# All low parts of the experts' weight slices on VectorE, and the selection mask by eight 16-bit comparisons

## The chip, the cores and the metric

The kernel runs on one core of a Trainium2 chip. Its metric is the device time of one execution in microseconds (us), as a median over runs. The engines are TensorE (PE in the profile; PEld is its weight load), VectorE (DVE), ScalarE (ACT), GpSimd (POOL) and SyncE (SP), which issues most of the DMA transfers.

## What is computed

One layer of a network over 1024 tokens of 1024 channels: a token mixer (gated delta rule in both directions and pooling), a projection, and then a mixture of experts, after which the result is normalised. The change lies almost wholly in the mixture of experts. It has 16 experts; each takes the 128 tokens that have the largest affinity to it, and puts them through three matrices of 1024 x 1024 in 32-bit floats (201 MB in all):

```python
def expert_choice_ffn(h, w_router, w_gate, w_up, w_down):
    B_, L, D = h.shape
    cap = EC_CAPACITY * L // N_EXPERTS                       # 128
    aff = jax.nn.softmax((h @ w_router).astype(jnp.float32), axis=-1)
    top_aff, top_idx = lax.top_k(jnp.swapaxes(aff, 1, 2), cap)
    xe = jax.vmap(lambda hb, ib: hb[ib])(h, top_idx)
    hid = jax.nn.silu(jnp.einsum('becd,edf->becf', xe, w_gate)) * jnp.einsum('becd,edf->becf', xe, w_up)
    ye = jnp.einsum('becf,efd->becd', hid, w_down) * top_aff[..., None].astype(h.dtype)
    combine = lambda ib, yb: jnp.zeros((L, D), yb.dtype).at[ib.reshape(-1)].add(yb.reshape(-1, D))
    return jax.vmap(combine)(top_idx, ye)
```

## The kernel before

A product of 32-bit matrices is made on TensorE from two parts of each operand: a high part, which is the operand rounded to the narrower format that TensorE multiplies in (fp32r), and a low part, which is what the rounding left. Three products are summed: high by high, high by low, low by high.

**Slices.** A weight matrix is taken in slices of 128 rows by 1024 columns (512 KB), eight to a matrix and 384 in all. The list `seq` sets the order in which they are needed: after the first gate matrix, for each expert e its up matrix, the gate matrix of expert e + 1, and its down matrix. These 24 slices are called a cycle here. SyncE loads slices into a ring of 34 places (tiles `rawa`, `oa`, `rawb`); a place takes its next slice once its present one has been split.

**Splitting.** `split_slice` (L1503 to L1517) makes the two parts of the next slice of the list: ScalarE copies it to the high part `fhi` (L1513), and then VectorE or GpSimd subtracts the high part from it and writes the low part `flo` (L1514). There are four buffers for each part. `use_slice` issues the six matmuls of a slice (L1632: two halves of 512 columns by three products, the low part's in the middle), and then calls `split_slice` for the slice four further on. Which engine makes the low part is a rule on the slice's number i: GpSimd where i % 6 is 5 (four slices of a cycle), VectorE otherwise. The first four slices are split on GpSimd in an earlier stage, beside the search for the experts' thresholds; that is not touched.

**A cycle in the code.** `up_mm(e)` uses the eight slices of the up matrix. After the fourth, `transpose_split` makes the next expert's input: eight transposes on TensorE (L1668), the high part on ScalarE (L1670, tiles `lhs`), the low part on VectorE (L1671). After the eighth, `select(e + 2)` finds which tokens an expert takes: eight small matmuls with that expert's mask (L1644), four small operations on VectorE (L1648 to L1652: `sv`, `ix`, `af`, `af`); `gather` issues an indirect DMA from GpSimd (L1658, tile `xe`), which lands the rows for the expert after next; and `onehot(e + 3)` makes the next mask (L1614). Then VectorE multiplies the activated gate by the up products (L1726, tile `sg`). `gate_mm(e + 1)` uses four slices, `transpose_split` transposes `sg`, and `gate_mm` uses the other four. `down_mm(e)` uses eight, and `scatter(e)` weights the result on VectorE (L1736, `ye`) and adds it to the output in DRAM by an indirect DMA from GpSimd (L1738, `accd`).

Each engine runs its instructions in the order in which the code issues them.

**The mask.** For each of eight tiles of 128 tokens, `oh[:, t, :]` holds a one where a token (a partition) has a slot (a column, 1 to 128) of the expert. `posT[:, t, e]` is a token's slot for expert e, or 0. One comparison over 8 x 128 elements makes it from two 32-bit operands, both broadcast. The mask itself is in 16 bits (bf16). The first mask is made from a tile in PSUM and the others from `posT`.

**A constant.** `slots` (the numbers 1 to 128 on each partition) is made on GpSimd ahead of the output projection, in a row of other constants; behind them GpSimd has a small operation for the output's norm (L1080, `ro`), whose result VectorE needs (L1082).

Of the kernel before, what the change touches and what calls it, by code (L numbers as in the profile page):

```python
# [7 lines left out]
F32 = mybir.dt.float32  # L8
F32R = mybir.dt.float32r
BF16 = mybir.dt.bfloat16  # L10
# [10 lines left out]
NT = 8  # L21
# [31 lines left out]
def trunk_kernel(ctx, tc, x, c, ctxt, c_ctx, w_mod, b_mod, norm1, norm2, w_in, conv_w, a_log, dt_bias,  # L53
# [12 lines left out]
    # ---------------------------------------------------------------- constants  # L66
# [17 lines left out]
    # parameter rows -> per-partition columns  # L84
# [13 lines left out]
    # inverse window sizes of the box means along rows and columns  # L98
# [14 lines left out]
    # ---------------------------------------------------------------- modulation and normalised inputs  # L113
# [97 lines left out]
    def prefetch(load=True):  # L211
        """split the next column block, then load the one after"""
        i = pos[0]
        pos[0] += 1
        if i < len(cols):
            split[i] = w_split(*cols[i])
        if load and i + 1 < len(cols):
            w_load(*cols[i + 1])
# [40 lines left out]
    def more_gemv():  # L259
        """the rest of the modulation, in steps"""  # L260
        for i, b in enumerate(MG):
            yield from gemv_steps(b, PSK, lambda: PSK.tile([128, 4, 128], F32, name="gtp"))
            if i + 2 < len(MG):
                gemv_load(MG[i + 2])
            if i < 2:
                yield
# [3 lines left out]
    # tokens: first in xnT, how many, first in their own part, row of the modulation, their part  # L270
    GROUPS = {"x": (LC, L, 0, 0, hx), "A": (LC, 512, 0, 0, hx), "B": (LC + 512, 512, 512, 0, hx), "c": (0, LC, 0, 1, hc)}
    # for four of the eight channel tiles, the steps of the modulated inputs: in place as they are (a), and as two
    # parts, high (h, or H from what is in place) and low (l, by DVE or POOL)
# [22 lines left out]
    # ---------------------------------------------------------------- input projection, convolution, pooling  # L296
# [5 lines left out]
    def project_ab(ks):  # L302
        """the decay and step columns, four parts of the sum side by side (32 columns each)"""
        if not ab_px:
            ab_px.extend(PSK.tile([128, 512], F32, name=f"ab{t}") for t in range(2))
            ab_px.append(PS2.tile([128, 4, 128], F32, name="tp").rearrange("p a b -> p (a b)")[:, 0:LC])
        for dst, n in zip(ab_px, (LC, LC + 512, 0)):
            m = dst.shape[1]
            for k in ks:
                j = k % 4  # L310
                PE.matmul(dst[32 * j:32 * j + 32], wab[:, k, :], xnT[:, k, n:n + m], start=(k < 4), stop=(k >= 4),
                          tile_position=(0, 32 * j))
# [14 lines left out]
    # [tile, channel, gate heads and pool groups, token]  # L327
# [4 lines left out]
    def delta_setup():  # L332
        """decays and step sizes of all chunks"""
# [56 lines left out]
    def copy2(t, dst, src):  # L390
        """two halves on two engines"""
        if t:
            DVE.tensor_copy(dst, src)
        else:
            ACT.activation(dst, src, AF.Copy)
# [3 lines left out]
    def rows_tile(ct, i):  # L399
        """where group i of a channel tile's tokens is transposed"""  # L400
# [6 lines left out]
    def conv_post(ct, px, pc, dst, after):  # L407
        """convolution and silu of channel tile ct, then what follows; in steps"""
# [103 lines left out]
    # keep the array's clock up until the first of these inputs is there  # L512
# [3 lines left out]
    # the products of the first block of keys as their inputs come: with the high parts (h), with the low parts (l)  # L516
# [39 lines left out]
    # eg[:, 0]: decay up to a token, 1: from it to the chunk's end, 2: of the whole chunk  # L556
# [35 lines left out]
    # ---------------------------------------------------------------- v and q; the chunks' inverses of the delta rule  # L592
# [8 lines left out]
    def masked_decays(cj):  # L601
        """log decays of the chunk's tokens in the columns of the tokens that they act on"""
# [11 lines left out]
    # a chunk's inverse ([lane][direction]) and decays on their way to DRAM  # L614
# [14 lines left out]
    def prep(cj, lane):  # L629
        """inverse and masked scores of chunk cj (0, 1: context) for both directions"""  # L630
# [118 lines left out]
    def k_scales():  # L749
        """step sizes over the keys' squared norms, once these are known"""  # L750
# [9 lines left out]
    def advance_preps():  # L760
        """the next stage of one of the chunks' inverses that are under way"""
# [40 lines left out]
    def pool_post(g, px):  # L802
        """difference to the box mean, mixed within the group"""
# [65 lines left out]
    # ---------------------------------------------------------------- gated delta rule, both directions  # L869
    OA = pools.push("oa")  # L870
    # the tiles in the order of their output projection, two to a buffer, which then holds experts' weights
# [25 lines left out]
    def scores(cj):  # L897
        """masked, decayed products of the chunk's queries and keys"""
# [11 lines left out]
    def scan(cjs, is_first, last):  # L910
        """one step of both directions: chunk cjs[d] for direction d"""
# [7 lines left out]
        def mm(lhs, rhs):  # L919
            """four products, one per head"""  # L920
            p = sc()
            for h in range(H):
                PE.matmul(p[:, h, :], lhs(h), rhs(h), start=True, stop=True)  # L923
            return p
# [104 lines left out]
    # ---------------------------------------------------------------- parts of the output projection, some ahead of it  # L1029
# [3 lines left out]
    def alt(t):  # L1033
        """tiles in turn use the buffers of two pools"""
# [17 lines left out]
    def wo_split(k):  # L1052
        """the parts of a block of rows times the gate"""
# [62 lines left out]
    def prefetches():  # L1116
        """what the output projection needs first, between the steps of the delta rule"""
# [50 lines left out]
    # ---------------------------------------------------------------- output projection, gated residual, router  # L1168
# [7 lines left out]
    # the order in which the experts' weights are needed: (expert, gate / up / down); the last but one's down after  # L1176
    # the last one's up
# [8 lines left out]
    # slices that for once lie in places of other tiles, loaded once the ring is full  # L1186
# [8 lines left out]
    def ring_b():  # L1195
        """the ring's places that the stage before frees last come last"""
# [47 lines left out]
    def y_mm(t, ks, hfs=(0, 1)):  # L1244
        """the last tile's halves lie in buffers of their own"""
# [13 lines left out]
    def residual(t, hf=None):  # L1259
        """x1 = x + y; the gate is in y's weights"""  # L1260
# [6 lines left out]
    def x1_norm(t, part=None):  # L1267
        """1 / rms; for one half of the columns after the other, or all at once"""
# [39 lines left out]
    def router_last(t, ks):  # L1308
        """the last tile's, on shorter a way"""
# [20 lines left out]
    def ffn_input(t):  # L1330
        """modulated input of the experts; x1 starts the sum of their outputs"""
# [16 lines left out]
    # partition (t, e) -> same expert; earlier tiles of the same expert  # L1348
# [11 lines left out]
    # search for the threshold: of each three candidates the first two, and for ScalarE the third one's negative plus  # L1360
    # half a unit, above the first value; their changes from digit to digit; the steps; the limits' negatives
# [18 lines left out]
    # token number and affinity (three exact parts) of every token  # L1380
# [10 lines left out]
    POOL.iota(slots, pattern=[[1, 128]], base=1, channel_multiplier=0, allow_small_or_imprecise_dtypes=True)  # L1391
    late = []
    for i in range(NT):
        t = [ORDER[j] if 0 <= j < NT else None for j in (i, i + 1, i + 2, i - 1)]
        if i == 0:
# [7 lines left out]
            # what the last tiles need lies where the next stage's first loads don't go  # L1403
# [86 lines left out]
    # ---------------------------------------------------------------- expert choice: the CAP largest per expert  # L1490
# [9 lines left out]
    # the places of what is needed late lie where the last stage's tiles are  # L1500
# [4 lines left out]
    def split_slice(eng=None):  # L1505
# [8 lines left out]
        (eng or (POOL if i % 6 == 5 and 5 < i < NS - 4 else DVE)).tensor_tensor(lo, raw, hi.bitcast(F32), op=OP.subtract)  # L1514
# [18 lines left out]
    # the threshold's bits, two at a time: bits 29..16, then bits 15..0 of the values that share them  # L1533
# [12 lines left out]
    def search(key, dst, nxt, unit, n):  # L1546
        """largest first + i * unit (i < 4 ** n) that at least CAP keys of the expert reach; the keys are multiples of unit

        of each three candidates, ScalarE counts for the last one the keys above less the keys below; nxt has them
        without the last digit's share d"""  # L1550
# [37 lines left out]
    # all above the threshold, and as many of the equal ones, from the first token on, as there is room for  # L1588
# [23 lines left out]
    def onehot(e, pos=None):  # L1612
        oh = FE.tile([128, NT, 128], BF16, name="oh", bufs=1)
        DVE.tensor_tensor(oh, slots[:, None, :].to_broadcast([128, NT, 128]),  # L1614
                          (posT if pos is None else pos)[:, :, e:e + 1].to_broadcast([128, NT, 128]), op=OP.is_equal)
# [6 lines left out]
    # ---------------------------------------------------------------- experts  # L1622
# [38 lines left out]
    def transpose_split(src, e):  # L1661
        """the two parts of a transposed operand of expert e; its input's and its hidden one's share buffers"""
# [33 lines left out]
    def transpose_onehot(e):  # L1696
        """the expert's selection with the slots on the partitions"""
# [71 lines left out]
    # ---------------------------------------------------------------- the last expert's outputs and the final norm  # L1769
# [12 lines left out]
    def final_sum(t):  # L1782
        """the last expert's outputs on top of the others'; TensorE adds some tiles', VectorE the others'"""
# [61 lines left out]
```

## Time and profile before

| | |
|---|---|
| median of 3 runs | 1383.76 us (1383.68 to 1389.02) |
| span of the profiled execution, first to last instruction | 1383.9 us |
| TensorE matmuls busy | 1260.0 us, 91% of the span |
| VectorE busy | 1020.7 us, 74% |
| ScalarE busy | 750.0 us, 54% |
| GpSimd busy | 564.1 us, 41% |
| DMA | 328.39 MB, mean 237 GB/s |

The profile is of one execution. It gives that execution's span and no time outside it, so the span is read as its own time; it is 0.1 us from the median. The shares are averages over stages with different limits, so what a change in the experts' stage is worth is read from that stage: from about 760 us to 1356 us, of which nearly all is a repetition of the cycle described above.

### The profile page before, as it was taken

How to read it: one execution, taken by the hardware profiler on the slowest of the kernel's cores; microseconds unless marked ns; L12 is line 12 of the kernel's file. 1: busy time of each engine (PE TensorE's matmuls, PEld its weight loads, DVE VectorE, ACT ScalarE, POOL GpSimd, SP SyncE). 2: the span in 40 equal slices, each digit the busy share in tenths (PEclk: the TensorE clock that was granted, in tenths of full speed). 3: DMA queues.
4: the chain of work that ended last, by engine and by line, in shares of the span. 5: the costliest groups of instructions: out<-in, count | busy, mean ns of one | idle time of the engine just before them, and what ended most of it. 6: DMA issues, size and time to landing. Idle time of an engine off the chain costs nothing.

```text
span 1383.9 us, 26524 instructions
## 1 busy us (share of the span) xinstructions
PE 1260.0 (91%) x10355; PEld 994.4 (72%) x10355; DVE 1020.7 (74%) x1606; ACT 750.0 (54%) x1103; POOL 564.1 (41%) x455
## 2 busy tenths in 40 slices
PE   5899898989999989989952999999999999999997
PEld 3476777766767779978842777777777777777884
DVE  4763675575775446845667889999999999999885
ACT  5443433343433335233232777777777777777783
POOL 5701543494845125651152333434334434443332
PEclk9999999999999999999975999999999999999999
DMA  9657213212223278436793899999999999999806
GB/s 355 211 195 257 69 37 101 73 48 79 73 68 108 78 262 302 168 129 223 260 342 128 282 310 365 363 371 370 363 364 367 366 363 369 367 368 358 322 3 256
DMA packets 140760, 328.39 MB, mean 237 GB/s; under 512 B 13517, under 2 KB 53082, under 8 KB 140634
## 3 DMA queue, kind: packets, MB, share of 16 engines
q1 hardware_dynamic: 134826, 305.72, 60.8%
q0 software_dynamic: 5376, 19.40, 5.4%
q8 instruction: 81, 1.33, 0.4%
q10 hardware_dynamic: 432, 1.57, 0.3%
q14 instruction: 45, 0.37, 0.1%
HBM read 287.32 MB, written 39.32 MB: 236 GB/s over the span
## 4 chain that ended last, share of the span: by engine, by line
PE 61%; DVE 18%; issue 8%; POOL 4%; DMA 4%; ACT 3%; SPq 0%; DVEq 0%; POOLq 0%; ACTq 0%
PE pd L1632 12%; PE pu L1632 11%; PE px L484 11%; DVE flo L1514 6%; PE y L1256 6%; PE pg L1632 5%; PE sc L923 4%; PE iv L687 2%; DVE acc L428 2%; PE tp L1668 1%; DVE sg L1726 1%; DMA wm<-in_w_mod_dram 1%; PE gv L132 1%; ACT fhi L1513 1%; DMA Vd<-rows 1%
## 5 line engine op out<-in xcount | busy, mean ns | idle before, releaser
L1514 DVE TENSOR_TENSOR flo<-rawb,fhi 128x1024 fp32r<-128x1024 f32 x147 | 207.4, 1457 | 26.4 <-ACT fhi L1513 26.2
L484 PE MATMUL px<-hx,whi 128*128 128x512 f32 x640 | 221.0, 425 | 4.5 <-ACT hx L290 2.7
L1513 ACT ACTIVATE fhi<-rawb 128x1024 fp32r<-128x1024 f32 x176 | 186.0, 1061 | 65.2 <-PE pg L1632 31.7
L1514 DVE TENSOR_TENSOR flo<-rawa,fhi 128x1024 fp32r<-128x1024 f32 x133 | 184.0, 1428 | 26.5 <-ACT fhi L1513 25.4
L1513 ACT ACTIVATE fhi<-rawa 128x1024 fp32r<-128x1024 f32 x158 | 166.9, 1061 | 60.0 <-PE pg L1632 32.0
L1632 PE MATMUL pg<-fhi,lhs 128*128 128x512 f32 x544 | 157.7, 402 | 0.0
L1632 PE MATMUL pu<-fhi,lhs 128*128 128x512 f32 x512 | 146.7, 398 | 0.0
L484 PEld LDWEIGHTS px<-hx,whi 128*128 128x128 f32 x640 | 112.7, 192 | 39.6 <-issue 11.3
L1514 POOL TENSOR_TENSOR flo<-rawb,fhi 128x1024 fp32r<-128x1024 f32 x29 | 75.6, 2606 | 144.7 <-ACT fhi L1513 78.0
L1632 PE MATMUL pd<-fhi,lhs 128*128 128x512 f32 x480 | 134.2, 396 | 0.0
L1514 POOL TENSOR_TENSOR flo<-rawa,fhi 128x1024 fp32r<-128x1024 f32 x29 | 74.8, 2581 | 134.3 <-ACT fhi L1513 65.4
L484 PE MATMUL px<-hx,wlo 128*128 128x512 f32 x320 | 128.5, 402 | 0.0
L1632 PEld LDWEIGHTS pg<-fhi,lhs 128*128 128x128 f32 x544 | 100.5, 189 | 22.5 <-ACT lhs L1670 0.4
L1632 PEld LDWEIGHTS pu<-fhi,lhs 128*128 128x128 f32 x512 | 95.0, 188 | 21.8
L1632 PEld LDWEIGHTS pd<-fhi,lhs 128*128 128x128 f32 x480 | 90.1, 188 | 21.6
L1632 PE MATMUL pg<-flo,lhs 128*128 128x512 f32 x272 | 87.2, 402 | 15.7 <-DVE flo L1514 15.7
L201 POOL TENSOR_TENSOR wlo<-wraw,whi 128x1024 fp32r<-128x1024 f32 x16 | 40.1, 2503 | 125.8 <-ACT whi L200 125.8
L1632 PE MATMUL pu<-flo,lhs 128*128 128x512 f32 x256 | 80.5, 395 | 0.0
L1256 PE MATMUL y<-ohi,mx 128*128 128x512 f32 x256 | 76.0, 402 | 0.8 <-DVE oa L981 0.8
L1632 PE MATMUL pd<-flo,lhs 128*128 128x512 f32 x240 | 75.5, 396 | 0.0
L1632 PEld LDWEIGHTS pg<-flo,lhs 128*128 128x128 f32 x272 | 50.3, 189 | 32.7 <-DVE flo L1514 21.4
L484 PEld LDWEIGHTS px<-hx,wlo 128*128 128x128 f32 x320 | 61.5, 192 | 14.1
(454 smaller groups left out, 2471.4 us busy)
## 6 DMA issues: line engine op xcount, KB each, us to landing
rawb<-in_w_down_dram SPq DMA_DIRECT2D x61, 512.0 KB, 8.0
rawb<-in_w_gate_dram SPq DMA_DIRECT2D x58, 512.0 KB, 5.5
rawb<-in_w_up_dram SPq DMA_DIRECT2D x57, 512.0 KB, 6.3
rawa<-in_w_gate_dram SPq DMA_DIRECT2D x56, 512.0 KB, 5.6
rawa<-in_w_up_dram SPq DMA_DIRECT2D x54, 512.0 KB, 5.7
rawa<-in_w_down_dram SPq DMA_DIRECT2D x52, 512.0 KB, 7.0
wm<-in_w_mod_dram SPq DMA_DIRECT2D x48, 512.0 KB, 6.7
wraw<-in_w_in_dram SPq DMA_DIRECT2D x20, 512.0 KB, 4.6
```

The lines of the kernel that those rows point to most:

```text
L132: PE.matmul(ps[32 * j:32 * j + 32], cs[:, k, :], t[:, i, :], start=(q < 2), stop=(q >= 2), tile_position=(0, 32 * j))
L201: (POOL if pos[0] > 4 else DVE).tensor_tensor(lo[:, :, :n], raw[:, :, :n], hi[:, :, :n].bitcast(F32), op=OP.subtract)
L428: DVE.scalar_tensor_tensor(acc, pad[:, j:j + L], convw(j, ct), acc, op0=OP.mult, op1=OP.add)
L484: PE.matmul(dst, wp[:, k, :], src[hp][:, k, o], start=start and i == 0, stop=stop and i == len(parts) - 1)
L687: PE.matmul(iv[r, u, o:64], pa[r, u, :], PV[r, u, o:64], start=True, stop=True)
L923: PE.matmul(p[:, h, :], lhs(h), rhs(h), start=True, stop=True)
L1256: PE.matmul(ys[t, hf][:, hf, :], l_[:, k, :], r_[:, 512 * hf:512 * hf + 512], start=(k == KORD[0] and i == 0), stop=(k == KORD[-1] and i = ...
L1513: ACT.activation(hi, raw, AF.Copy)
L1514: (eng or (POOL if i % 6 == 5 and 5 < i < NS - 4 else DVE)).tensor_tensor(lo, raw, hi.bitcast(F32), op=OP.subtract)
L1632: PE.matmul(ps[:, hf, :], l_[:, k, :], r_[:, 512 * hf:512 * hf + 512], start=(k == 0 and n == 0), stop=(k == KD - 1 and n == 2))
L1668: PE.transpose(tp[:, q, :], src[:, 128 * k:128 * k + 128], ident)
L1726: DVE.tensor_tensor(gs[e], gs[e], pu.pop(e).rearrange("p a b -> p (a b)"), op=OP.mult)
```

## The change

Three edits. In `split_slice` the rule that gives every sixth low part to GpSimd is taken out, so that VectorE makes all of them. In `onehot` the one comparison of 8 x 128 elements becomes eight comparisons of 128 elements, each of a 16-bit copy of the slot numbers with one 32-bit number per partition (the first mask stays as it was). The 16-bit copy, `slotb`, is a new tile and one more operation on GpSimd. The rest of the full diff takes comments and docstrings out.

```diff
     slots = WS.tile([128, 128], F32, name="slots")
     POOL.iota(slots, pattern=[[1, 128]], base=1, channel_multiplier=0, allow_small_or_imprecise_dtypes=True)
+    slotb = WS.tile([128, 128], BF16, name="slotb")
+    POOL.tensor_copy(slotb, slots)
...
         if i >= SPLITS:
             ACT.activation(hi, raw, AF.Copy)
-        (eng or (POOL if i % 6 == 5 and 5 < i < NS - 4 else DVE)).tensor_tensor(lo, raw, hi.bitcast(F32), op=OP.subtract)
+        (eng or DVE).tensor_tensor(lo, raw, hi.bitcast(F32), op=OP.subtract)
...
     def onehot(e, pos=None):
         oh = FE.tile([128, NT, 128], BF16, name="oh", bufs=1)
-        DVE.tensor_tensor(oh, slots[:, None, :].to_broadcast([128, NT, 128]),
-                          (posT if pos is None else pos)[:, :, e:e + 1].to_broadcast([128, NT, 128]), op=OP.is_equal)
+        if pos is not None:
+            DVE.tensor_tensor(oh, slots[:, None, :].to_broadcast([128, NT, 128]),
+                              pos[:, :, e:e + 1].to_broadcast([128, NT, 128]), op=OP.is_equal)
+        else:
+            for t in range(NT):
+                DVE.tensor_scalar(oh[:, t, :], slotb, posT[:, t, e:e + 1], None, op0=OP.is_equal)
         ohs[e] = oh
```

On VectorE, in one cycle, around the mask (the first rows are low parts made beside the last up slices; `rawb` and `rawa` are places of the ring), before:

```order
L1514 TENSOR_TENSOR flo<-rawb_8897,fhi 128x1024
L1514 TENSOR_TENSOR flo<-rawb_8909,fhi 128x1024
L1648 COPY sv<-tp 128x5
L1649 SCALAR_TENSOR_TENSOR ix<-sv,tp 128x1
L1651 TENSOR_TENSOR af<-sv 128x1
L1652 TENSOR_TENSOR af<-af,sv 128x1
L1614 TENSOR_TENSOR oh<-slots,posT 128x1024
L1726 TENSOR_TENSOR sg<-sg,pu 128x1024
L1514 TENSOR_TENSOR flo<-rawb_8921,fhi 128x1024
L1514 TENSOR_TENSOR flo<-rawb_8943,fhi 128x1024
L1514 TENSOR_TENSOR flo<-rawa,fhi 128x1024
L1671 TENSOR_TENSOR lhs_9483<-tp,lhs_9482 128x512 x2
```

The same place in the changed kernel, where buffers and lines are numbered anew:

```order
L1516 TENSOR_TENSOR flo<-rawb_8908,fhi 128x1024
L1516 TENSOR_TENSOR flo<-rawb_8920,fhi 128x1024
L1516 TENSOR_TENSOR flo<-rawb_8932,fhi 128x1024
L1654 COPY sv<-tp 128x5
L1655 SCALAR_TENSOR_TENSOR ix<-sv,tp 128x1
L1657 TENSOR_TENSOR af<-sv 128x1
L1658 TENSOR_TENSOR af<-af,sv 128x1
L1621 TENSOR_SCALAR oh<-slotb,posT 128x128 x8
L1732 TENSOR_TENSOR sg<-sg,pu 128x1024
L1516 TENSOR_TENSOR flo<-rawb_8944,fhi 128x1024
L1516 TENSOR_TENSOR flo<-rawb_8966,fhi 128x1024
L1516 TENSOR_TENSOR flo<-rawa,fhi 128x1024 x2
```

Ahead of the four small operations VectorE now has three low parts where it had two, and between `sg` and the `lhs` pair four where it had three; the mask is eight rows' worth of instructions instead of one.

On GpSimd, from the four early splits to the first scatters (`xe` is a gather, `accd` a scatter), before:

```order
L1514 TENSOR_TENSOR flo<-rawa,fhi 128x1024 x4
L1658 DMA xe<-h2d,ix 128x1024 x2
L1514 TENSOR_TENSOR flo<-rawa,fhi 128x1024
L1514 TENSOR_TENSOR flo<-oa_7863,fhi 128x1024
L1658 DMA xe<-h2d,ix 128x1024
L1514 TENSOR_TENSOR flo<-rawb_8095,fhi 128x1024
L1514 TENSOR_TENSOR flo<-rawb_8085,fhi 128x1024
L1514 TENSOR_TENSOR flo<-rawb_8089,fhi 128x1024
L1738 DMA accd<-ye,ix 1024x1024
```

and in the changed kernel:

```order
L1516 TENSOR_TENSOR flo<-rawa,fhi 128x1024 x4
L1664 DMA xe<-h2d,ix 128x1024 x3
L1744 DMA accd<-ye,ix 1024x1024
L1664 DMA xe<-h2d,ix 128x1024
L1744 DMA accd<-ye,ix 1024x1024
```

GpSimd keeps nothing in the experts' stage but the issue of the gathers and scatters. On the same engine, ahead of the output projection, the changed kernel has one row more, the copy to 16 bits in front of the norm's `ro`:

```order
L1385 IOTA jpp 128x1
L1386 CAST vals<-jt 128x128
L1387 CAST vals<-jpp 128x128
L1391 IOTA slots 128x128
L1393 CAST slotb<-slots 128x128
L1080 TENSOR_TENSOR ro<-ro,mhalf 128x4
```

The order on TensorE, ScalarE and SyncE is as before.

## Rows read from the trace of the kernel before

**Rows 1.** The page's first line.

```profile
span 1383.9 us, 26524 instructions
```

**Rows 2.** The chain that ended last, in order of time: start, us, what.

```profile
800.92 11.21 PE pd L1632 x48
...
1249.65 11.20 PE pd L1632 x48
...
1285.30 11.20 PE pd L1632 x48
```

**Rows 3.** TensorE's waits, 755 to 1300 us: total, times, longest.

```profile
PE pg L1632 <- DVE flo L1514: 15.7, 13, 1.4
```

**Rows 4.** Timeline of TensorE: start, us, what; first and last cycle with a selection.

```profile
785.02 0.71 PE L1632 MATMUL pg<-fhi,lhs 128*128 128x512 f32 x2
...
799.88 0.38 PE L1069 MATMUL tp<-ident,modT 128*128 128x128 f32 x2
...
1272.98 0.71 PE L1632 MATMUL pg<-fhi,lhs 128*128 128x512 f32 x2
...
1278.66 1.03 PE L1668 MATMUL tp<-ident,sg 128*128 128x128 f32 x8
...
1280.01 0.63 PE L1632 MATMUL pg<-flo,lhs 128*128 128x512 f32 x2
```

**Rows 5.** Timeline of VectorE in one cycle: start, us, what.

```profile
874.20 5.75 DVE L1514 TENSOR_TENSOR flo<-rawa,fhi 128x1024 fp32r<-128x1024 f32 x5
...
898.75 3.32 DVE L1514 TENSOR_TENSOR flo<-rawb,fhi 128x1024 fp32r<-128x1024 f32 x2 [1.34 <-ACT fhi L1513]
...
902.51 1.22 DVE L1614 TENSOR_TENSOR oh<-slots,posT 128x1024 bf16<-128x1024 f32 x1
903.65 1.21 DVE L1726 TENSOR_TENSOR sg<-sg,pu 128x1024 f32<-128x1024 f32 x1
904.78 5.70 DVE L1514 TENSOR_TENSOR flo<-rawb,fhi 128x1024 fp32r<-128x1024 f32 x3
```

**Rows 6.** Timeline of GpSimd in that cycle, and one row of the last.

```profile
897.46 2.39 POOL L1514 TENSOR_TENSOR flo<-rawb,fhi 128x1024 fp32r<-128x1024 f32 x1 [4.33 <-issue]
902.61 1.98 POOL L1658 DMA_INDIRECT xe<-h2d,ix  x1 [2.76 <-DVE af L1651]
906.15 3.24 POOL L1514 TENSOR_TENSOR flo<-rawb,fhi 128x1024 fp32r<-128x1024 f32 x1 [1.57 <-ACT fhi L1513]
...
1276.52 0.98 POOL L1658 DMA_INDIRECT xe<-h2d,ix  x1 [2.75 <-DVE af L1651]
```

**Rows 7.** Line L1514: duration ns min/median/max, first and last start us.

```profile
L1514 DVE TENSOR_TENSOR flo<-rawa,fhi x133: 1205/1212/3432, 764.2 to 1352.1; 128x1024 fp32r<-128x1024 f32 x133
...
L1514 POOL TENSOR_TENSOR flo<-rawb,fhi x29: 2391/2432/3276, 792.1 to 1333.6; 128x1024 fp32r<-128x1024 f32 x29
```

**Rows 8.** Timeline of VectorE, comparisons and the like on 128 elements.

```profile
77.93 0.22 DVE L345 TENSOR_SCALAR lsr<-jp 128x128 fp32r<-128x128 int32 x1
78.06 0.22 DVE L344 TENSOR_SCALAR mi<-jp 128x128 f32<-128x128 int32 x1
...
592.45 0.40 DVE L1355 TENSOR_SCALAR pmod<-jp 128x128 int32<-128x128 int32 x1 [0.20 <-POOL jp L1350]
...
734.58 0.29 DVE L1585 TENSOR_SCALAR khi<-khi,thr 128x128 f32<-128x128 f32 x1
```

**Rows 9.** The chain that ended last, ahead of the output projection.

```profile
603.20 0.35 POOL vals L1387
...
604.70 0.70 DVE oa L1082
```

**Rows 10.** Three stretches: us, each engine's busy us, granted clock, DMA share, GB/s.

```profile
800.00:1300.00 500.00, 484.57 (x2257) 385.72 (x2256) 453.05 (x413) 378.41 (x391) 197.16 (x80) 1.00 1.00 365
1280.00:1300.00 20.00, 20.00 (x87) 16.14 (x86) 17.57 (x15) 16.05 (x17) 7.96 (x3) 1.00 1.03 410
1310.00:1352.00 42.00, 42.00 (x200) 34.10 (x200) 37.27 (x32) 34.19 (x37) 12.62 (x5) 1.00 0.08 13
```

## The prediction

> **What bounds the kernel now.** I read the chain that ended last first, for where the time repeats. In the experts' stage it returns to the first down product of each expert: from 800.92 to 1249.65 us in twelve cycles, 37.39 us each, and then a last one of 35.65 us, to 1285.30 [rows 2]. Both hold 24 slices, two transpositions and a selection; the last one alone makes no mask. Next I read TensorE's waits, for what it lacks: the low part of a gate slice, 13 times, 15.7 us [rows 3]. Twelve of these lie in the twelve cycles and one ahead of them. In the last cycle there is none, and TensorE is busy without a gap from 1280 to 1300 us [rows 10]. So TensorE is the bound, a cycle without a wait is 35.65 us, and each cycle with a mask loses 1.74 us.
>
> Third, VectorE's timeline in one such cycle, for why the low part is late [rows 5]. Left alone it makes five low parts in 5.75 us, which is 1.136 us from one to the next (five steps and 0.07 us of overlap). But two take 3.32 us from 898.75, and three 5.70 us from 904.78. Beside each of these runs a low part of GpSimd's, 897.46 to 899.85 and 906.15 to 909.39 [rows 6]. The view of the line L1514 says how they meet: VectorE's operation takes 1.21 us in the median and 3.43 at most, GpSimd's 2.43 and 3.28 at most [rows 7]. One holds the other up for most of its length. The two trains lose 1.0 and 2.2 us so, and the train of three is the one that TensorE waits for.
>
> **The change, part by part.** I count from the first gate matmul behind the up products: 1272.98 in the last cycle [rows 4], and ten cycles of 37.39 us earlier, 899.08, in the one shown. TensorE's needs come from the last cycle, which has no wait [rows 4]: `sg` by 5.68 for its transposition; the first low part behind it by 7.03, and then one every 1.40 us (eight slices take 11.20 [rows 2]): 8.43, 9.83, 11.23, and the first of the down slices by 12.63.
>
> *Low parts.* VectorE gets four more per cycle, 4 x 1.136 = 4.5 us, and loses the times in which GpSimd holds it up. At the train of two: the low part that was GpSimd's is now made on VectorE at 897.4, in an idle stretch (1.34 us idle ahead of 898.75 [rows 5]). The two behind it need 2.3 us instead of 3.32; the second waits for ScalarE's part, so that the small operations start at 2.25 instead of 2.93.
>
> *Mask.* One operation now, 1.14 us from start to start (902.51 to 903.65). Eight of 128 elements: the nearest rows are two comparisons of a 128 x 128 tile with 0.22 us each and 0.13 us from start to start [rows 8]. They have 32-bit elements and a constant; a number per partition may cost more, as the comparison of 0.29 us at 734.58 has, which less the same overlap of 0.08 us is 0.21. Lower bound 0.07 us each (nothing but the overlap's length), upper bound 0.40 (the longest row of this form and size, at 592.45). I take 0.135, so 1.08 us in all; the mask as such gains nothing.
>
> *The lump.* Small operations 2.25 to 2.77 (0.52 us, from 898.75 + 3.32 less overlap to 902.51); mask to 3.85; `sg`, 1.13 us from start to start, to 4.98, wanted at 5.68. Then four low parts, GpSimd's former one among them: 6.12, 7.25, 8.39, 9.53, wanted at 7.03, 8.43, 9.83, 11.23. Then the `lhs` pair, 1.20 us, and the first low part for the down slices at 11.87, wanted at 12.63. Nothing is late; the least room is 0.70 us, at `sg`. Before, the third of the train ended at 11.4 and was wanted at 9.83, which is the 1.5 us of the wait; the rest of the 1.74 is `sg`, 0.2 us late. Behind the instructions that VectorE gains stand the `lhs` pair and `ye`; `ye` comes after one more low part, but its scatter stood behind that same low part on GpSimd before, so it leaves about as early as it did.
>
> *Over a cycle* VectorE has 24 x 1.136 + 2 x 1.20 + 0.52 + 1.08 + 1.13 + 1.20 (`ye`, by the row of `sg`) = 33.6 us in 35.65. Were every low part 1.21 us, with no overlap, it would be 35.4; still inside, but with nothing left.
>
> *Slot numbers in 16 bits.* The cast stands in front of `ro` on GpSimd, where the chain that ended last runs through GpSimd's constants, one of them a cast of the same size with 0.35 us, and on to the `oa` that waits for `ro` [rows 9]. So it is on the path, and costs 0.35 us; without that row it would be bounded by 0 and a whole low part's 2.43.
>
> *Sum.* Twelve cycles x 1.74 = 20.9. The first mask's stretch, ahead of the twelve, takes 14.86 us from 785.02 to 799.88 [rows 4], where the last cycle needs 12.3 (1272.98 to 1285.30 [rows 2]): 2.5 more. Less 0.35 for the cast: 23.1 us. From the span of 1383.9 [rows 1], that gives 1360.8; the median of the runs is 0.1 below the span. I predict **1361 us**. Its own range is 1359 to 1364: up to 3 us if the waits do not quite vanish.
>
> **The rivals.** *A. A gather holds the mask up.* The gather's issue on GpSimd takes 0.98 us beside `sg`, but 1.98 beside the one long mask [rows 6]: it waits for the mask and then runs. Between eight short comparisons it may get in and hold VectorE for its 0.98 us. For it: they start within 0.1 us of each other. Against it: there is only one such issue per cycle. Price: the room is 0.70 us on a mask of 1.08, so a mask of 1.78 costs nothing. With 0.98 more, a mask of 2.06 loses 0.28 us in 13 places, 1364.5; with comparisons of 0.21 us besides (2.66) it loses 0.88, 1372. The Trainium skill ("SBUF — State Buffer", Who interferes with whom) says that a tensor_scalar in a two-port mode and GpSimd's writing of descriptors lock each other out, and that whichever starts first holds the port for its whole instruction. No row here has such a pair; by that rule this case holds at every gather.
>
> *B. The comparisons are long, with no gather in them.* At 0.29 us each with no overlap the mask is 2.32 us and 0.54 is lost in 13 places: 1368.
>
> *C. Slower: they are longer still.* Each instruction pays a start. From 0.44 us each the mask (3.52 us) takes back all of the 1.74; at 0.50 it takes 2.22 in 13 places against 1.74, 1390. For it: the 0.40 us row. Against it: the other rows are half of that, and the 0.40 one does another operation.
>
> *D. No change: the loads become the bound.* The DMA engines show a share of 1.00 and 365 GB/s from 800 to 1300 us [rows 10]; 365 over 37.39 us is 13.6 MB a cycle, and 35.65 us would need 383. If 365 were the limit, the place of the wait would move to the loads. Against it: 410 GB/s for 20 us from 1280; and the loads end by 1310, while the low parts go on to 1352 [rows 7, 10], so that the ring is more than 40 us ahead, which 23 us cannot use up. The time would be 1384. The Trainium skill ("DMA: Bandwidth & Descriptors", Where 436 GB/s comes from) gives about 358 GB/s as the share of HBM for one core. By that, nothing is to be had here. The 410 GB/s of this trace contradicts it for a core that runs alone.
>
> **How the numbers follow.** A measurement of this kernel can tell 0.5%, about 7 us, from no change. Forecast 0.62; A 0.12; B 0.09; D, or another wait that takes the place of the old one, 0.10; C 0.07. Forecast, A and B are faster by over 0.5%, 0.83; D is within it, 0.10; C is slower, 0.07. The range goes from 1357 (a little below the forecast's own, should the low parts get shorter throughout) to 1374, which takes in A and B.
>
> **What would show it.** If it is right, the chain goes from one first down product to the next in 35.6 to 35.9 us thirteen times; TensorE's waits for `flo` behind the gate matmuls are gone; the low parts on VectorE have a mean near their median of 1.21 us and no length near 3.4; GpSimd's rows are gathers and scatters alone; the eight comparisons start 0.10 to 0.15 us apart; `ro` is about 0.35 us later. A shows as a gap of about 1 us between two comparisons, B and C as their distance from start to start. D shows as waits of ScalarE or VectorE for a load of `rawa` or `rawb`. The prediction is wrong if TensorE waits elsewhere in the cycle, above all at the first down slices, where the low parts have 0.8 us to spare, or if low parts of far over 1.21 us remain without GpSimd's.

## The result and the profile after

The changed kernel takes **1362.75 us** in the median of four runs (1360.88 to 1365.92), against 1383.8 for four runs of the one before (1383.68 to 1389.02): a ratio of 0.9839, 95% interval 0.982 to 0.9859. That is 21.0 us faster; 1361 was predicted, with a range of 1357 to 1374. The profiled execution is the longest of the four; the spans of the others were 1359.9, 1359.2 and 1362.2 us.

First the page: its first line and the busy time of each engine.

```profile
span 1364.2 us, 26631 instructions
...
PE 1261.2 (92%) x10355; PEld 1003.4 (74%) x10355; DVE 1029.5 (75%) x1773; ACT 751.1 (55%) x1103; POOL 390.6 (29%) x394
```

VectorE has taken over 62 low parts and is busy for only 9 us more (1020.7 before), while GpSimd lost 174 us (564.1 before). 62 low parts at 1.16 us (the mean of this trace, below) are 72 us; by this estimate, some 63 us of VectorE's busy time before had been time in which it was held up.

The chain that ended last, in order of time (start, us, what), has the first down product of each expert at an even distance:

```profile
802.36 11.21 PE pd L1638 x48
838.01 11.20 PE pd L1638 x48
...
1229.95 11.20 PE pd L1638 x48
1265.57 11.20 PE pd L1638 x48
```

That is thirteen cycles of 35.63 us, where twelve had 37.39 and one 35.65 [rows 2]. TensorE's waits for `flo` [rows 3] are gone: between 802 and 1285 us that view has no row at all. Two stretches (us, busy us of TensorE, its weight load, VectorE, ScalarE and GpSimd, granted clock, DMA share, GB/s) show the same:

```profile
800.00:1300.00 500.00, 500.00 (x2356) 404.92 (x2355) 481.56 (x571) 395.42 (x409) 45.72 (x27) 1.00 0.99 372
...
1240.00:1260.00 20.00, 20.00 (x102) 16.25 (x102) 19.23 (x22) 16.13 (x17) 3.29 (x2) 1.00 1.03 378
```

TensorE is busy for all of the 500 us (484.57 before [rows 10]), at the same granted clock of 1.00 (the upper of its two levels). VectorE is at 96%.

The operations of the experts' stage by line (count, duration in ns as least, median and longest, first and last start) are the low parts by place of the ring, the comparisons and the gathers.

```profile
L1516 DVE TENSOR_TENSOR flo<-rawb,fhi x176: 1216/1225/1231, 789.3 to 1319.4; 128x1024 fp32r<-128x1024 f32 x176
L1516 DVE TENSOR_TENSOR flo<-rawa,fhi x158: 1216/1225/1233, 767.6 to 1332.3; 128x1024 fp32r<-128x1024 f32 x158
...
L1621 DVE TENSOR_SCALAR oh<-slotb,posT x120: 243/249/485, 756.3 to 1221.5; 128x128 bf16<-128x128 bf16 x120
...
L1664 POOL DMA_INDIRECT xe<-h2d,ix x16: 969/1032/1091, 757.2 to 1256.6; - x16
```

No low part takes longer than 1.23 us (3.43 before [rows 7]), and no gather's issue longer than 1.09 (1.98 beside the mask before [rows 6]). One cycle on VectorE, where [rows 5] was before; the first gate matmul behind the up products starts at 896.97 here:

```profile
898.05 1.23 DVE L1516 TENSOR_TENSOR flo<-rawb,fhi 128x1024 fp32r<-128x1024 f32 x1 [0.17 <-ACT fhi L1515]
899.19 0.16 DVE L1654 COPY sv<-tp 128x5 f32<-128x5 f32 x1
...
899.72 1.61 DVE L1621 TENSOR_SCALAR oh<-slotb,posT 128x128 bf16<-128x128 bf16 x8
901.02 1.22 DVE L1732 TENSOR_TENSOR sg<-sg,pu 128x1024 f32<-128x1024 f32 x1
902.15 4.63 DVE L1516 TENSOR_TENSOR flo<-rawb,fhi 128x1024 fp32r<-128x1024 f32 x4
906.69 1.29 DVE L1677 TENSOR_TENSOR lhs<-tp,lhs 128x512 fp32r<-128x512 f32 x2
907.88 9.35 DVE L1516 TENSOR_TENSOR flo<-rawb,fhi 128x1024 fp32r<-128x1024 f32 x8
```

The lump is as it was foreseen, a mask of eight rows and a train of four low parts, with other sizes: the mask takes 1.30 us from start to start (899.72 to 901.02), and eight low parts 9.35. TensorE and GpSimd at this place:

```profile
902.64 1.03 PE L1674 MATMUL tp<-ident,sg 128*128 128x128 f32 x8
```

```profile
888.68 2.29 POOL L1744 DMA_INDIRECT accd<-ye,ix  x1 [23.01 <-DVE ye L1742]
900.28 1.03 POOL L1664 DMA_INDIRECT xe<-h2d,ix  x1 [9.30 <-PE pg L1638]
```

`sg` is done at 902.24 and wanted at 902.64, so 0.40 us are left. The gather's issue begins in the midst of the eight comparisons and ends at 901.31. The last comparison, which alone would have been done at about 901.1, ends at 901.33, just behind it. It is so in all 13 masks of this trace that a gather's issue meets from 790 us on: one comparison, the last, takes 0.44 to 0.49 us where the others take 0.25, and ends 0.01 to 0.02 us behind the issue. So the issue does hold one comparison up, by some 0.2 us; `sg` starts on time all the same, and this costs nothing.

**Where the 19.7 us between the two spans lie.** From the first down product to the fourteenth: 463.21 us (802.36 to 1265.57) for 484.38, 21.2 less. From the first gate matmul behind the first mask (789.05) to the transposes ahead of the first down product (801.32): 12.27 us for 14.86 [rows 4], 2.6 less. Against these 23.8 us stands a first gate matmul that starts 4.0 us later, at 789.05 for 785.02. Of this, 0.36 is the cast, which the chain shows on the path (from the start of the last `vals` to that of `oa` 1.86 us, for 1.50 [rows 9]):

```profile
605.28 0.35 POOL vals L1387
605.63 0.11 POOL slots L1391
605.80 0.29 POOL slotb L1393
606.09 1.02 POOL ro L1080
607.14 0.70 DVE oa L1082
```

Of the other 3.7 us, 2.1 lie ahead of the cast, where the two kernels are the same (605.28 for 603.20 [rows 9]), and most of the rest between it and the first mask, where they are the same as well. The traces of the kernels below differ there too: in all but those of 8 and 9, which change that stage, the first down product starts between 795.8 and 803.7 us.

### The profile page after: what moved, and what is told of

Read it like the earlier page. It is cut to its first block, busy times and chain, and to the rows that moved or that the text cites. A ratio compares the mean times of both kernels' runs of the same rounds, so it can differ in the third digit from the quotient of the medians.

```text
span 1364.2 us, 26631 instructions
## 1 busy us (share of the span) xinstructions
PE 1261.2 (92%) x10355; PEld 1003.4 (74%) x10355; DVE 1029.5 (75%) x1773; ACT 751.1 (55%) x1103; POOL 390.6 (29%) x394
## 4 chain that ended last, share of the span: by engine, by line
PE 75%; DVE 11%; issue 4%; POOL 4%; DMA 3%; ACT 2%; SPq 0%; POOLq 0%; ACTq 0%; DVEq 0%
PE pg L1638 14%; PE pu L1638 13%; PE pd L1638 12%; PE px L484 11%; PE y L1256 6%; PE sc L923 5%; PE iv L687 2%; DVE acc L428 2%; PE tp L1674 2%; PE gv L132 1%; DMA wm<-in_w_mod_dram 1%; DVE pT L666 1%; DMA Vd<-rows 1%; PE pc L484 1%; DVE T L704 1%
## 5 line engine op out<-in xcount | busy, mean ns | idle before, releaser
L1516 DVE TENSOR_TENSOR flo<-rawa,fhi 128x1024 fp32r<-128x1024 f32 x158 | 187.3, 1224 | 12.9 <-ACT fhi L1515 12.2
L1744 POOL DMA_INDIRECT accd<-ye,ix x15 | 34.6, 2310 | 366.2 <-DVE ye L1742 366.2
L428 DVE SCALAR_TENSOR_TENSOR acc<-pad,prmT,acc 128x1024 f32<-128x1024 f32 x36 | 66.3, 1843 | 3.6 <-ACT acc L424 3.3
L1664 POOL DMA_INDIRECT xe<-h2d,ix x16 | 16.4, 1027 | 168.7 <-PE pg L1638 120.7
```

The lines of the kernel that those rows point to most:

```text
L428: DVE.scalar_tensor_tensor(acc, pad[:, j:j + L], convw(j, ct), acc, op0=OP.mult, op1=OP.add)
L1516: (eng or DVE).tensor_tensor(lo, raw, hi.bitcast(F32), op=OP.subtract)
L1664: POOL.indirect_dma_start(out=xe[e], out_offset=None, in_=h2d[:, :], in_offset=bass.IndirectOffsetOnAxis(ap=ix[:, 0:1], axis=0))
L1744: POOL.indirect_dma_start(out=accd[:, :], out_offset=bass.IndirectOffsetOnAxis(ap=idx.pop(e)[:, 0:1], axis=0), in_=ye, in_offset=None, com ...
```

## The experiments

They ask three things: which edit gave the time, whether what gave it is that GpSimd and VectorE hold each other up, and how much room the cycle has left. The median of the changed kernel, 1362.75, is the mark; ratios are to the kernel before, run beside each.

**1. The low parts alone** (mask and constant as before; the diff is against the kernel before).

```diff
-        (eng or (POOL if i % 6 == 5 and 5 < i < NS - 4 else DVE)).tensor_tensor(lo, raw, hi.bitcast(F32), op=OP.subtract)
+        (eng or DVE).tensor_tensor(lo, raw, hi.bitcast(F32), op=OP.subtract)
```

> The low parts all on VectorE, the mask by one comparison as before, and no 16-bit copy of the slot numbers. Theory (GpSimd's low parts hold VectorE's up, and that is the whole loss): no wait of TensorE for a low part, cycles of 35.6 us, 1360 to 1363 us, 0.4 below the full change for want of the cast. Rival (the shorter mask is what brought the gain): waits as before, 1384 us.

1363.05 us (1359.77 to 1364.7), ratio 0.9848 [0.9828, 0.9868]; cycles of 35.63 us, no wait for `flo`. The whole gain is here. Mask and cast add nothing to it that can be told from the spread of the runs.

**2. The mask alone** (eight comparisons and cast; low parts divided as before).

```diff
-        (eng or DVE).tensor_tensor(lo, raw, hi.bitcast(F32), op=OP.subtract)
+        (eng or (POOL if i % 6 == 5 and 5 < i < NS - 4 else DVE)).tensor_tensor(lo, raw, hi.bitcast(F32), op=OP.subtract)
```

(This diff and those of 3 to 9 are against the changed kernel.)

> The mask by eight comparisons and the cast, the low parts divided as before. Theory: the mask's 1.30 us in place of 1.14 adds to a lump that is already late, 13 x 0.16 = 2 us and 0.4 for the cast, 1386 to 1388 us. Rival (the mask brought the gain): 1362 us.

1373.03 us (1368.58 to 1374.65), ratio 0.991 [0.9884, 0.9937]. Theory and rival both miss: the mask alone brings about half, 0.9% of 1.6%. TensorE's waits (total, times, longest) have no row for `flo` any more:

```profile
PE tp L1674 <- DVE sg L1732: 4.3, 13, 1.0
```

A cycle is 36.22 us, which is two thirds of the way from 37.39 to 35.63. VectorE and GpSimd in one of them:

```profile
866.36 1.21 DVE L1732 TENSOR_TENSOR sg<-sg,pu 128x1024 f32<-128x1024 f32 x1
867.50 2.35 DVE L1516 TENSOR_TENSOR flo<-rawb,fhi 128x1024 fp32r<-128x1024 f32 x2
869.77 1.22 DVE L1516 TENSOR_TENSOR flo<-rawa,fhi 128x1024 fp32r<-128x1024 f32 x1
```

```profile
865.15 1.01 POOL L1664 DMA_INDIRECT xe<-h2d,ix  x1 [2.76 <-DVE af L1657]
868.71 4.54 POOL L1516 TENSOR_TENSOR flo<-rawa,fhi 128x1024 fp32r<-128x1024 f32 x1 [2.54 <-ACT fhi L1515]
```

The hold-up is still there, but it has changed sides. The train of three runs free, and GpSimd's low part stretches to 4.54 us: it ends at 873.25, 2.3 us behind the train (870.99), so it waited for the train and then ran. In the kernel before, GpSimd got in ahead of the third [rows 5, 6].

**3 and 4. Two of GpSimd's four low parts kept**: those beside the down products, or those beside the up and gate products around the mask.

```diff
-        (eng or DVE).tensor_tensor(lo, raw, hi.bitcast(F32), op=OP.subtract)
+        (eng or (POOL if i % 24 in (5, 11) and 5 < i < NS - 4 else DVE)).tensor_tensor(lo, raw, hi.bitcast(F32), op=OP.subtract)
```

> GpSimd keeps two of its four low parts in a cycle, those made beside the down products; VectorE has the two beside the mask. Theory (only the hold-ups beside the mask matter): no wait of TensorE for a gate slice, 1362 to 1364 us, though some low parts on VectorE still reach 3 us. Rival (what counts is VectorE's sum over a cycle): half the gain, about 1373 us, as the opposite half.

1363.25 us (1358.72 to 1366.18), ratio 0.9836 [0.9807, 0.9866]; cycles of 35.63, no wait for `flo`. These two cost nothing, so the sum of VectorE's work is not what counts, but the place. With `(17, 23)` in place of `(5, 11)`:

> The opposite half: GpSimd keeps the two low parts beside the mask, VectorE has those beside the down products. Theory: the waits for the gate's low part are as before, 13 of 1.4 us, 1382 to 1387 us. Rival (VectorE's sum over a cycle): about 1373 us.

1371.8 us (1367.84 to 1373.4), ratio 0.9911 [0.9893, 0.993]; cycles of 36.22 us and 4.2 us of waits for `sg`, as in experiment 2. The place is right and the size missed, for the same reason as there. The rival's number agrees, but by its reason (VectorE's sum) the run before would have lost time too.

**5. GpSimd made to read again**: beside VectorE's, it repeats its four low parts in pieces into a tile that nobody reads any more.

```diff
+        if i % 6 == 5 and 5 < i < NS - 4:
+            for q in range(4):
+                f = slice(256 * q, 256 * q + 256)
+                POOL.tensor_tensor(slots.bitcast(BF16), raw[:, f], hi.bitcast(F32)[:, f], op=OP.subtract)
```

> All of the change, and GpSimd makes its former four low parts of a cycle once more, in four pieces of 256 columns, into a tile that nobody reads. VectorE's own work and order are those of the full change. Theory (operations of GpSimd that read SBUF hold VectorE's low parts up): each of the four costs VectorE 1.2 to 2.4 us, 4.8 to 9.6 a cycle against 1.4 to spare, so TensorE waits again and the time is 1400 to 1470 us, slower than before. Rival (what mattered was where the low parts stand in the two engines' orders): 1363 us.

1442.43 us (1439.18 to 1444.2), ratio 1.042 [1.0388, 1.0453]. VectorE's low parts now have a median of 1.39 to 1.75 us, by place of the ring, for 1.22, and TensorE waits for it at two places:

```profile
PE tp L1678 <- DVE sg L1736: 24.1, 13, 1.9
PE pd L1642 <- DVE flo L1516: 8.0, 12, 0.7
```

These two rows are 32 of the 80 us. VectorE is now busy for 497.3 of the 500 us from 800 to 1300, so it sets TensorE's pace throughout, not only where the view shows a wait. A piece of 256 columns takes GpSimd 1.37 us, so four of them keep it longer than its low part did (2.43 us [rows 7]): this run is more than the old state brought back.

**6. GpSimd made to write only**, at the same four places, eight fills of 128 x 256 each.

```diff
+        if i % 6 == 5 and 5 < i < NS - 4:
+            for q in range(8):
+                POOL.memset(slots.bitcast(BF16), 0.0)
```

> All of the change, and at the same four places eight memsets of 256 elements each on GpSimd, which write SBUF and read nothing. Theory (it is reading that collides): VectorE's low parts stay at 1.21 to 1.23 us, 1363 us. Rival (any operation of GpSimd in SBUF holds VectorE up): low parts of 1.5 us and more, over 1385 us.

1363.59 us (1360.31 to 1367.2), ratio 0.9845 [0.9813, 0.9877], cycles of 35.63. 496 operations of 0.33 us on GpSimd cost nothing. So it is GpSimd's reading of SBUF, and not that it works there, which holds VectorE up. This is what the Trainium skill ("SBUF — State Buffer", Who interferes with whom) says: a VectorE operation with two inputs in SBUF contends with a GpSimd operation that reads SBUF and not with one that only writes it. Experiments 5 and 6 agree.

**7. How much room is left: sixteen comparisons.**

```diff
-            for t in range(NT):
+            for t in [*range(NT), *range(NT)]:
```

> All of the change, with each mask written twice (sixteen comparisons). Theory (the room at the product behind the mask decides, 0.41 us in the changed kernel's trace): 1.30 us more are 0.9 us late in 13 places, 1370 to 1375 us. Rival (VectorE's sum over a cycle decides): 1.30 us fit into the 1.4 us that VectorE has to spare in a cycle, 1363 to 1365 us.

1374.13 us (1373.41 to 1378.3), ratio 0.9926 [0.9904, 0.9949]; 13 waits for `sg` of 0.89 us each (11.6 in all). 1.30 more of mask less 0.40 of room is 0.90. So the room at `sg` is what was read, and beyond it TensorE pays for each comparison.

**8 and 9. The first four low parts too**, behind the search for the thresholds on VectorE, where GpSimd made them beside it; first on top of the change, then with the old mask and without the cast.

```diff
-                if hf:
-                    split_slice(POOL)
...
     select(1, FE.tile([128, D], F32, name="g2b")[:, 0:8])
+    for _ in range(SPLITS):
+        split_slice()
```

> All of the change, and the first four slices' low parts too are made on VectorE, not beside the search for the thresholds but behind it, while TensorE waits for the first gather (VectorE is idle for 5.3 us there and four low parts take 4.6). Theory (in the search too GpSimd's low parts hold VectorE up, four times 2.0 to 2.2 us on the path): 8 us less, 1353 to 1357 us. Rival (the search is hidden, or the four low parts are late for the first gate slices): 1361 to 1364 us.

1354.87 us (1350.06 to 1357.81), ratio 0.9797 [0.9764, 0.9829].

> The version with all low parts on VectorE, the first four behind the search, the mask by one comparison and no cast. Theory: TensorE has no wait in the cycles and the search is 8 us shorter, as with the eight comparisons, 1353 to 1356 us. Rival (the eight comparisons are worth something of their own once the low parts are moved): 1357 to 1360 us.

1354.44 us (1350.68 to 1358.3), ratio 0.9773 [0.9732, 0.9814]. Beside GpSimd's four early low parts in the kernel before, the search's small operations take 2.18 to 2.51 us instead of 0.16 to 0.35:

```profile
724.26 0.23 DVE L1566 SCALAR_TENSOR_TENSOR nxt<-sgn,d,nxt 128x3 f32<-128x3 f32 x1
724.53 2.33 DVE L1567 TENSOR_TENSOR nxt<-nxt,dlt 128x3 f32<-128x3 f32 x1
...
726.97 2.18 DVE L1556 TENSOR_TENSOR c<-nxt,d 128x1 f32<-128x1 f32 x1
```

Four times some 2.1 us is the 8 us that both gain on the changed kernel. That both come out alike says once more that the eight comparisons add nothing once the low parts have moved.

**10 to 12. Why the mask alone brings half.** In experiment 2 the train starts 0.16 us later behind a longer mask; the gather's issue runs free; and the mask is of another form. Each of the next three kernels keeps GpSimd's four low parts and separates one of these. First the kernel before with the cast and one more comparison of 128 behind its mask:

```diff
             DVE.tensor_tensor(oh, slots[:, None, :].to_broadcast([128, NT, 128]),
                               posT[:, :, e:e + 1].to_broadcast([128, NT, 128]), op=OP.is_equal)
+            DVE.tensor_scalar(oh[:, 0, :], slotb, posT[:, 0, e:e + 1], None, op0=OP.is_equal)
```

> Low parts divided as before and the mask by one long comparison as before, with one comparison of 128 elements more behind it (and the cast). The run with eight comparisons alone gave 1373 us, where GpSimd's low part came 0.16 us earlier against VectorE's train of three and waited for the train instead of holding it up. Theory (it is a race for a turn, and 0.16 us of delay on VectorE decide it): GpSimd's low part beside the train takes 4.5 us instead of 3.24 and the cycle is 36.2 us, 1371 to 1375 us. Rival (the short comparisons do it, by letting the gather's issue through): the cycle is 37.4 to 37.6 us, 1384 to 1388 us.

1395.19 us (1390.83 to 1396.66), ratio 1.0067 [1.0045, 1.0089]: slower than before. GpSimd gets in again, and a late `sg` comes on top (waits of 18.7 us for `flo` and 5.9 for `sg`).

```profile
904.97 5.68 DVE L1516 TENSOR_TENSOR flo<-rawb,fhi 128x1024 fp32r<-128x1024 f32 x3
```

```profile
906.04 2.40 POOL L1516 TENSOR_TENSOR flo<-rawb,fhi 128x1024 fp32r<-128x1024 f32 x1 [1.54 <-ACT fhi L1515]
```

So the delay alone does not make GpSimd wait. But the run overshot: GpSimd starts 1.07 us behind the train's start here, where experiment 2 has 1.21, and gets in ahead of the second low part. It is the next run that puts the race to the test. It has the eight comparisons and a train that starts earlier, since it leaves the affinity's third part out (against experiment 2):

```diff
-        DVE.tensor_tensor(af, af, sv[:, 4:5], op=OP.add)
```

> Low parts divided as before, the mask by eight comparisons, and one small addition ahead of the mask left out (the affinity's third part is not added), so that the train of three starts 0.2 us earlier than in the run with eight comparisons alone, at about 5.65 after the first gate matmul, where it stood before (5.70). Theory (race for a turn): GpSimd's low part gets in between the second and the third of the train again, cycles of 37.2 to 37.4 us, 1381 to 1386 us. Rival (the short comparisons): 1369 to 1373 us.

1369.13 us (1365.99 to 1374.68), ratio 0.9887 [0.9843, 0.993]. The rival's number came: GpSimd waits as in experiment 2, though it starts 1.38 us behind the train's start, as in the kernel before (906.15 less 904.78 [rows 5, 6]):

```profile
900.84 3.49 DVE L1516 TENSOR_TENSOR flo<-rawb,fhi 128x1024 fp32r<-128x1024 f32 x3
```

```profile
902.22 4.38 POOL L1516 TENSOR_TENSOR flo<-rawb,fhi 128x1024 fp32r<-128x1024 f32 x1 [2.54 <-ACT fhi L1515]
```

With the same start against the train, the outcome is the other one, so the theory of a race fell.

Last, the kernel before with its long mask behind `sg` instead of ahead of it, so that the gather's issue does not meet it (against the kernel before):

```diff
-                if e + 3 < NX:
-                    onehot(e + 3)
...
         DVE.tensor_tensor(gs[e], gs[e], pu.pop(e).rearrange("p a b -> p (a b)"), op=OP.mult)
+        if e + 3 < NX:
+            onehot(e + 3)
```

> The kernel before, with its one long comparison issued behind the product sg instead of ahead of it. VectorE then runs sg, the mask and the train of three low parts; the train starts as late as before, and GpSimd's low part waits for ScalarE's high part as before, but the gather's issue now runs beside sg. Theory: a gather's issue that is held up by the long mask goes with GpSimd's low part getting in ahead of VectorE's third. Then the issue takes 0.98 us, GpSimd's low part 4.4 to 4.5 us, VectorE's train of three 3.5 us, no wait for flo is left, and a cycle is 35.7 to 36.2 us: 1362 to 1371 us. Rival: the held-up issue only goes along with the long mask. Then GpSimd's low part takes 3.2 us and the train 5.7 us as before, TensorE's waits for flo stay near 15 us over 12 cycles, and at most the 0.2 us of sg per cycle are saved: 1381 to 1384 us.

1384.93 us (1380.34 to 1388.8, 10 runs), against 1388.17 for the kernel before beside it; ratio 0.9989 [0.997, 1.0009]. This theory fell too: the issue is free, and GpSimd gets in all the same, 1.36 us behind the train's start:

```profile
898.49 1.22 DVE L1614 TENSOR_TENSOR oh<-slots,posT 128x1024 bf16<-128x1024 f32 x1
899.62 5.70 DVE L1514 TENSOR_TENSOR flo<-rawb,fhi 128x1024 fp32r<-128x1024 f32 x3
```

```profile
897.45 0.98 POOL L1658 DMA_INDIRECT xe<-h2d,ix  x1 [2.75 <-DVE af L1651]
900.98 3.26 POOL L1514 TENSOR_TENSOR flo<-rawb,fhi 128x1024 fp32r<-128x1024 f32 x1 [2.55 <-ACT fhi L1513]
```

So neither the delay nor the held-up issue decides it. What is left is the form of the mask in the same cycle: with the one long comparison GpSimd got in (the kernel before, experiments 10 and 12), with eight short ones it waited (2, 4 and 11). It is so in every cycle with a mask and not only in those shown: no low part of GpSimd takes longer than 3.28 us in the kernel before, in 10 and in 12, and in 11 those behind the mask take 4.35 us and more (the line of `rawb` in 11, in ns as least, median and longest):

```profile
L1516 POOL TENSOR_TENSOR flo<-rawb,fhi x29: 2396/2424/5075, 792.5 to 1316.0; 128x1024 fp32r<-128x1024 f32 x29
```

Why an operation that has ended should matter to the one after next stays open.

## Why the prediction was right

**The bound and the cause.** TensorE's cycle without a wait, 35.65 us, was read from the one cycle that had no wait, and it is now every cycle (35.63). That GpSimd's and VectorE's low parts hold each other up was the reason given; experiments 1, 5 and 6 show it, with this edit alone, with GpSimd's reading brought back, and with GpSimd at work but not reading. Experiment 3 narrows it: only the two low parts around the mask cost time.

**The sum.** Twelve cycles at 1.74 us and 2.5 for the first mask's stretch were 23.4 us; the trace has 23.8, from cycles 1.76 shorter and 2.6. The cast was put at 0.35 us and costs 0.36. The sum was made between spans, and the runs' times lie 1.7 us above their spans (1365.92 and 1364.2); the front of this document had read the span as the execution's time. In spans, 1360.8 was worked out, and the four measured have a median of 1361.05. That these agree so closely is in part luck: 23.1 us less was forecast, and 21.0 were measured between the medians. The profiled execution before, from whose span the 23.1 were taken, was about 1.8 us longer than the median run (1383.9 and 1.7 against 1383.8), and this made up for most of the difference.

**The wait before.** The prediction put TensorE's wait for the low part at 1.5 of the 1.74 us. The rows have 1.2 (15.7 us in 13 times [rows 3]). The sum used the cycle's whole loss, so it did not suffer.

**The mask** was the term that was mis-sized: 0.16 us from one comparison to the next and not 0.135, so 1.30 us and not 1.08. The row that gave 0.13 had a constant to compare with; the one taken for the upper side (0.21) was too long. It cost nothing, as 0.40 of the 0.70 us of room was left. The mask took 0.22 of it, and 0.08 was never there: the prediction took the start of the operation behind `sg` for the end of `sg`.

**Low parts and VectorE's load.** In a train without a gap a low part is 1.135 us from start to start (902.15 to 906.69 for four), as was worked out. But not all of them stand in such a train: in the train of eight that follows (9.35 us), the last one starts a little late. One that stands alone takes its whole 1.22 us, and over the thirteen cycles the mean is 1.16. With the longer mask, this puts VectorE at 96% where 33.6 of 35.65, 94%, was worked out.

**"The mask as such gains nothing"** held for the change as made, but not for the reason behind it. That counted only the mask's own length. Alone, it saves 0.9% by turning the hold-up on GpSimd (experiment 2). The two edits take away the same wait, so their gains don't add; had only the mask been changed, the same argument would have missed by half the gain.

**The rivals.** A: no gap of 1 us between comparisons; 16 issues took 1.09 us at most. The rule of the Trainium skill that was set beside it ("SBUF — State Buffer", Who interferes with whom) does not show here as it is put there, since neither side is held for the other's whole instruction; what shows is one comparison of 0.47 us instead of 0.25 that ends with the issue. B and C: 0.16 us, far from 0.29 and 0.44; experiment 7 shows their mechanism at the price that the room gives. D: 372 GB/s over the 500 us and 383 from 1200 to 1250, which is what 35.65 us need, with no wait of TensorE for a load in the cycles.

## What to carry to other kernels

Price a divided operation by what the two engines do to each other where they meet, not by what each does alone: here giving a sixth of the low parts to a less busy engine cost 21 us, all of it by the two in a cycle that stand around the mask; the two beside the down products cost nothing. Read the cycle without the wait from the trace, list what is wanted when, and put the least room beside the least certain price. Test two edits one at a time before adding their gains, since both may take away the same wait.

## What was not expected of the hardware

- Who gets the next turn is not set by start times alone: GpSimd's low part started 1.36 to 1.38 us behind the start of a train of three in the kernel before, in experiment 12 and in 11, and got in ahead of the third in the first two (the train took 5.70 us) and not in the last (3.49).
- A tiny VectorE operation can lose about as much as a large one: 128 x 1 took 2.18 us beside a GpSimd subtraction of 128 x 1024, and 0.16 alone; a low part of 128 x 1024 took up to 3.43 [rows 7], and 1.21 alone.
- A comparison of 128 x 128 in 16 bits with a number per partition takes 0.249 us, no less than the 0.22 us of the nearest 32-bit rows [rows 8], so the 16 bits bought nothing here that shows.
